# Loading the activation table set with exponential and logarithm in the output projection of a two-layer decoder kernel

## The chip, the cores and the metric

The kernel runs on one core of a Trainium2 chip (trn2). The metric is the device time of one execution in microseconds; the time before is the median of three runs.

## The reference

The reference is a decoder trunk of two layers on a sequence of 2048 real tokens with 16 learned meta tokens ahead of them, model width 1024, in float32. Every layer normalises, projects, attends, gates and projects back onto the residual stream.

```
for layer in range(2):
    hn = rmsnorm(h, norm_g[layer])
    if layer == 0:   # stick-breaking attention (8 heads) beside latent attention (8 heads)
        h = h + concat(o_sb * silu(g_sb), o_mla * silu(g_mla)) @ ev_w_out
    else:            # sliding window of 128, 16 heads, sinks and ALiBi
        h = h + (o * silu(g)) @ od_w_out
return rmsnorm(h, final_g)[:, 128:]
```

Here `rmsnorm(x, g)` is `x * rsqrt(mean(x*x) + 1e-6) * g`, and `silu(g)` is `g / (1 + exp(-g))`. The attention of layer 0 needs log-sigmoid, exponential and softmax; that of layer 1 a softmax with a sink.

## The kernel before, in words

Everything is one function, `build`, of a single program without loops on the device. It lays the sequence out as 17 blocks of 122 rows. Large products are made exact by splitting both factors into a rounded high part (float32r) and the remainder; every product is then three matmuls. A split is two instructions: a rounding copy on ACT or DVE, and a subtraction on POOL or DVE.

The work has these stages, by the time at which the profile shows them:

1. Norm and input projections of layer 0, up to about 600 us. The norm's reciprocal root is `rstd` (line 411): a logarithm on ACT (line 412) and an exponential of -0.5 times it (line 413). The gates are `silu` (line 435): on ACT an exponential (438), a logarithm (439) and an exponential (440).
2. The attention of layer 0, to about 1562 us. Its activations on ACT are Softplus (lines 1059, 1089, 1123) and Copy. The order of the instructions on PE, ACT, DVE and POOL is given by a planner (`list_schedule`).
3. The output projection of layer 0, from 1562 us. Here the order on PE, ACT, DVE, POOL and SP is the order of the program's text (`manual_schedule`, entered at line 1230). It begins with three blocks of rows at once (lines 1328 to 1345): eight steps k, each of which loads and splits one slice of the attention's result (`split_og`, line 1263: high part on ACT at line 1267, remainder on POOL at line 1268) and one slice of the weights (`split_w0`, line 1253: high parts on DVE, remainders on POOL at odd k and on DVE at even k), and then runs 18 matmuls (`out_mm`, lines 1273 to 1275). Slices are loaded two steps ahead over SP's queue into two buffers. Then follow the other 14 blocks in a fixed order of slots (lines 1346 to 1381): `step` loads and splits two more slices of the attention's result per call, `add` adds the residual on DVE, `scale` (line 1289) squares on ACT and calls `rstd`, `turn` transposes on PE and `place` (line 1301) scales, splits and stores into the operand of the next layer.
4. The projections of layer 1 for keys, values and queries (lines 1464 to 1551), to about 2010 us.
5. The windowed attention of layer 1 (lines 1559 to 1890), again in the order of the text on PE, ACT, DVE and POOL. It goes through 76 units (19 blocks of 108 queries, two halves, two groups of heads): scores on PE (lines 1598, 1599), their eviction on DVE with the row maximum (`mx`, line 1602), exponentials on ACT (line 1613), the product with the reciprocal sum on POOL (1622), transposes on PE (1632) with evictions on ACT (1635) and DVE (1637), and the product with the values on PE (1646). Between these steps `fill` puts matmuls of two other works from a queue, as many as a credit allows: first the gates of layer 1 (`gates`, line 1682, with the splits of the next weights in `w1_part` at lines 1417 on ACT and 1418 on DVE), then the output projection of layer 1 (`project`, line 1795). A gate's evacuation `gate_evac` (line 1692) is spread over the next ticks: line 1696 on DVE, the three activations below on ACT, and the product of line 1704 on DVE, which frees the gate's PSUM tile. Three such tiles exist.
6. The last rows: the final norm in `final` (line 1827) and, for the last block, `square` and `final_last` (lines 1807 to 1825), which again call `rstd`.

```
 411      def rstd(ss, n, scale):
 412          S.activation(ss[:n], ss[:n], AF.Ln, bias=epst[:n], scale=scale)
 413          S.activation(ss[:n], ss[:n], AF.Exp, scale=-0.5)

1698              def s2():
1699                  S.activation(g1[:, :n], g1[:, :n], AF.Exp)
1700                  S.activation(g1[:, :n], g1[:, :n], AF.Ln, bias=1.0)
1701                  S.activation(g1[:, :n], g1[:, :n], AF.Exp, scale=-1.0)
```

ACT takes its functions from the table set that is loaded. The first statement of `build`, line 370, loads one by name, `natural_log_exp_and_others`. Otherwise the text says nothing of tables: the loads that an activation needs are put in front of it when the program is built, and the profile shows each as an `ACT_TABLE_LOAD` on that activation's line.

Of the kernel before, what the change touches and what calls it, by code (L numbers as in the profile page):

```python
# [340 lines left out]
def build(tc, a, off, upto=99):  # L341
    nc = tc.nc
    V, S, G, T = nc.vector, nc.scalar, nc.gpsimd, nc.tensor
# [60 lines left out]
    def f(t):  # L404
        return t.bitcast(F32)

    def split(hi, lo, src, heng=None, leng=None):
        (heng or V).tensor_copy(hi, src)  # L408
        (leng or G).tensor_tensor(lo, src, f(hi), op=ALU.subtract)  # L409
# [816 lines left out]
    def part(c0):  # L1226
        return (*xA, 0) if c0 < HALF else (*xB, HALF)
# [11 lines left out]
    def load_x(b):  # L1239
        xt = xts[b] = tmp.tile([P, D], F32, tag="xt", name="xt")  # L1240
        if b == 0:
            G.memset(xt[0:32], 0.0)
            dma(xt[PAD:PAD + NMETA], a["meta"])
            dma(xt[PAD + NMETA:BK], a["x"][0, 0:BK - PAD - NMETA])
        else:
            r = b * BK - PAD - NMETA
            dma(xt[:BK], a["x"][0, r:r + BK])

    def load_w0(k):
        raws["w", k] = tmp.tile([P, D], F32, tag="xt", name="raw")  # L1250
        dma(raws["w", k], wout[:, k])

    def split_w0(k):
        raw = raws.pop(("w", k))
        for j in range(2):
            split(*wo[j][k], raw[:, 512 * j:512 * (j + 1)], leng=(G if k % 2 else V))

    def load_og(g, k):
        n = (QG[g][1] - QG[g][0]) * BK
        raws[g, k] = tmp.tile([P, 512], F32, tag="raw", name="raw")[:, :n]  # L1260
        dma(raws[g, k], d_og[g][:, k])

    def split_og(g, k):
        c0, c1 = QG[g][0] * BK, QG[g][1] * BK
        h, l, o = part(c0)
        raw, h, l = raws.pop((g, k)), h[:, k, c0 - o:c1 - o], l[:, k, c0 - o:c1 - o]
        S.activation(h, raw, AF.Copy)
        G.tensor_tensor(l, raw, f(h), op=ALU.subtract)

    def out_mm(b, j, k):  # L1270
        h, l, o = part(b * BK)
        r, ps = slice(b * BK - o, (b + 1) * BK - o), pss[b][:, j]
        T.matmul(ps[:BK], h[:, k, r], wo[j][k][0], start=(k == 0), stop=False)
        T.matmul(ps[:BK], h[:, k, r], wo[j][k][1], start=False, stop=False)
        T.matmul(ps[:BK], l[:, k, r], wo[j][k][0], start=False, stop=(k == KT - 1))
# [56 lines left out]
        pss[b] = ps_v.tile([P, 2, 512], F32, tag="o", name="pso")  # L1332
    for k in range(KT):
        split_og(4, k)
        split_w0(k)
        if k + 2 < KT:
            load_og(4, k + 2)
            load_w0(k + 2)
        else:
            loaded.append(pieces.pop(0))  # L1340
            load_og(*loaded[-1])
            load_x(first[k + 2 - KT])
        for b in first:
            for j in range(2):
                out_mm(b, j, k)
# [574 lines left out]
```

## Time and profile before

| | |
|---|---|
| median of 3 runs | 2607.51 us (2605.27 to 2611.18) |
| the profiled execution | 2609.1 us, its span 2607.3 us |
| mean granted clock of PE | 0.99 |
| PE busy | 2541.9 us, 97% of the span |
| ACT busy | 1492.2 us, 57% |
| DVE busy | 1533.2 us, 59% |
| POOL busy | 1038.9 us, 40% |
| DMA, share of 16 engines on the main queue | 45.3% |

The span is the time from the first to the last instruction of the profiled execution; its time is a little longer. PE is TensorE's matmuls and PEld its weight loads, which overlap; ACT is ScalarE, DVE VectorE, POOL GpSimd, SP the engine that issues most DMAs. Busy time is that of instructions; a matmul's end is modelled, so a busy PE is not PE at its peak. A view of waits names an instruction, behind an arrow the one that released it, and then the us waited in total, how often, and the longest. In a list of instructions in order of time each line has the start in us, the duration in us, engine, line and what it writes from what; idle time in front of it, with its releaser, stands in brackets. The granted clock is the share of full speed that PE was allowed.

### The profile page before, as it was taken

How to read it: one execution, taken by the hardware profiler on the slowest of the kernel's cores; microseconds unless marked ns; L12 is line 12 of the kernel's file. 1: busy time of each engine (PE TensorE's matmuls, PEld its weight loads, DVE VectorE, ACT ScalarE, POOL GpSimd, SP SyncE). 2: the span in 40 equal slices, each digit the busy share in tenths (PEclk: the TensorE clock that was granted, in tenths of full speed). 3: DMA queues.
4: the chain of work that ended last, by engine and by line, in shares of the span. 5: the costliest groups of instructions: out<-in, count | busy, mean ns of one | idle time of the engine just before them, and what ended most of it. 6: DMA issues, size and time to landing. Idle time of an engine off the chain costs nothing. (4 is left out here: it accounts for less than half of the span.)

```text
span 2607.3 us, 38925 instructions
## 1 busy us (share of the span) xinstructions
PE 2541.9 (97%) x13105; PEld 1975.7 (76%) x13105; DVE 1533.2 (59%) x3356; ACT 1492.2 (57%) x3492; POOL 1038.9 (40%) x846
## 2 busy tenths in 40 slices
PE   9999999999999999999999999999999899999998
PEld 7888988899966666666665657788999788767776
DVE  5365496778335665565575664333222576888984
ACT  6542121213268878878878773644222999976564
POOL 1011201000068778878878775200000223445551
PEclk9999999999999999999999999999999999999999
DMA  5476734342594352261331115526454444666653
GB/s 146 111 200 178 205 95 117 90 123 68 138 196 107 87 141 67 71 155 47 81 95 36 49 55 168 150 85 161 119 123 118 107 118 126 166 188 191 200 150 100
DMA packets 337858, 321.30 MB, mean 123 GB/s; under 512 B 143670, under 2 KB 319738, under 8 KB 337075
## 3 DMA queue, kind: packets, MB, share of 16 engines
q1 hardware_dynamic: 336939, 317.56, 45.3%
q8 instruction: 103, 1.69, 0.3%
q10 hardware_dynamic: 720, 1.26, 0.1%
q14 instruction: 96, 0.79, 0.1%
HBM read 198.28 MB, written 120.80 MB: 122 GB/s over the span
## 5 line engine op out<-in xcount | busy, mean ns | idle before, releaser
L1622 POOL TENSOR_TENSOR s_sb<-s_sb,den 108x1008 f32<-108x1008 f32 (+1 forms) x76 | 147.6, 1942 | 548.7 <-DVE den L1621 456.0
L1079 POOL TENSOR_TENSOR l<-sp,h 123x488 fp32r<-123x488 f32 (+3 forms) x253 | 294.0, 1168 | 109.0 <-DVE h L1074 88.3
L1074 DVE CAST h<-sp 123x488 fp32r<-123x488 f32 (+3 forms) x266 | 177.7, 673 | 258.5 <-ACT sp L1066 232.8
L1137 POOL TENSOR_TENSOR acc<-acc,p 122x488 f32<-122x488 f32 (+3 forms) x288 | 313.4, 1108 | 31.4 <-DVE p L1129 24.2
L419 PE MATMUL psd<-xh,wh 128*128 128x366 f32 (+1 forms) x760 | 274.2, 361 | 0.0
L420 PE MATMUL psd<-xl,wh 128*128 128x366 f32 (+1 forms) x760 | 267.8, 352 | 0.0
L421 PE MATMUL psd<-xh,wl 128*128 128x366 f32 (+1 forms) x760 | 267.8, 352 | 0.0
L1059 ACT ACTIVATE sp<-zp 123x488 f32<-123x488 f32 (+3 forms) x360 | 173.1, 515 | 63.7 <-PE zp L1048 30.9
L1089 ACT ACTIVATE a<-zp 123x488 f32<-123x488 f32 (+3 forms) x360 | 168.2, 503 | 40.7 <-PE zp L1085 24.0
L1066 ACT ACTIVATE sp<-zp 1x488 f32<-1x488 f32 (+3 forms) x320 | 154.3, 496 | 40.3 <-PE zp L1085 36.3
L1613 ACT ACTIVATE s_sb<-s_sb,nm 108x252 f32<-108x252 f32 (+1 forms) x304 | 149.2, 494 | 36.7 <-DVE nm L1604 36.7
L1123 ACT ACTIVATE p<-ms 122x488 f32<-122x488 f32 (+3 forms) x320 | 150.6, 513 | 23.6 <-PE mav L1145 21.3
L420 PEld LDWEIGHTS psd<-xl,wh 128*128 128x128 f32 x760 | 144.1, 190 | 15.9 <-issue 0.9
L419 PEld LDWEIGHTS psd<-xh,wh 128*128 128x128 f32 x760 | 144.0, 190 | 12.5 <-issue 0.7
L421 PEld LDWEIGHTS psd<-xh,wl 128*128 128x128 f32 x760 | 143.5, 189 | 10.9
L1047 PEld LDWEIGHTS zp<-q,kbig 128*123 128x123 f32 x320 | 58.9, 184 | 113.1 <-ACT a L1089 60.5
L1145 PE MATMUL mav<-p,mvbig 122*64 122x488 f32 (+3 forms) x640 | 142.8, 524 | 0.0
L1097 PE MATMUL av<-a,vbig 123*64 123x488 f32 (+3 forms) x640 | 142.4, 523 | 0.0
L1079 DVE TENSOR_TENSOR l<-sp,h 123x488 fp32r<-123x488 f32 (+3 forms) x107 | 131.4, 1234 | 16.8 <-ACT h L1072 13.2
L409 POOL TENSOR_TENSOR wl<-raw,wh 128x1024 fp32r<-128x1024 f32 x17 | 40.9, 2404 | 244.9 <-DVE wh L408 159.0
L1047 PE MATMUL zp<-q,kbig 128*123 128x488 f32 (+3 forms) x320 | 127.3, 401 | 8.5 <-DMA kbig<-d_sk 5.2
L1602 DVE CUSTOM_DVE_ANT_0 s_sb<-pss,bt,sinks 108x252 f32<-108x252 f32 (+1 forms) x304 | 127.3, 473 | 12.2 <-PE pss L1599 4.3
(518 smaller groups left out, 6995.4 us busy)
## 6 DMA issues: line engine op xcount, KB each, us to landing
kbig<-d_sk SPq DMA_DIRECT2D x32, 492.0 KB
q<-d_q SPq DMA_DIRECT2D x36, 432.0 KB
xt<-in_x SPq DMA_DIRECT2D x32, 448.0 KB
raw<-in_od_w_in SPq DMA_DIRECT2D x48, 256.0 KB
mq<-d_mq SPq DMA_DIRECT2D x32, 373.6 KB
raw<-in_ev_w_in SPq DMA_DIRECT2D x19, 512.0 KB
kkb<-d_kk SPq DMA_DIRECT2D x18, 472.0 KB
xt<-d_h SPq DMA_DIRECT2D x16, 512.0 KB
```

Source lines behind the costliest of these rows:

```text
L419: T.matmul(o, wh[:, k, m0:m1], xh[:, k, c0:c1], start=(k == 0), stop=False)
L420: T.matmul(o, wh[:, k, m0:m1], xl[:, k, c0:c1], start=False, stop=False)
L421: T.matmul(o, wl[:, k, m0:m1], xh[:, k, c0:c1], start=False, stop=(k == k_n - 1))
L1047: T.matmul(zp[:BC, :s.ns], k[:, 2 * m, c], q, start=True, stop=False)
L1059: S.activation(sp[:BC, :s.ns], s.zp[m][:BC, :s.ns], AF.Softplus)
L1066: S.activation(s.sp[m][0:1, n - k:n], s.prev.zp[m][0:1, :k], AF.Copy, scale=-1.0 / CW)
L1074: V.tensor_copy(h[:BC, :n], sp[:BC, :n])
L1079: on_(on).tensor_tensor(l[:BC, :n], s.sp[m][:BC, :n], f(s.h[m][:BC, :n]), op=ALU.subtract)
L1089: S.activation(x[:BC, :s.ns], s.zp[m][:BC, :s.ns], AF.Softplus)
L1123: S.activation(pt[:BK, :s.nm], s.ms[m][:BK, :s.nm], AF.Softplus, scale=MSC)
L1137: eng.tensor_tensor(g.acc[m][:BK, s.jm:g.n], g.acc[m][:BK, s.jm:g.n], s.pt[m][:BK, :n], op=ALU.add)
L1613: S.activation(s_sb[:nq, hh, :ww], s_sb[:nq, hh, :ww], AF.Exp, bias=nm[:nq, hh:hh + 1], scale=SLOPES[h], accum_out=den[:nq, hh:hh + 1])
```

## The change

One statement is put into the first loop of the output projection. Behind ACT's first split of the attention's result (k = 0) and ahead of the second, ACT loads the same table set as at line 370.

```
     for k in range(KT):
         split_og(4, k)
+        if k == 0:
+            S.preload_act_table_set("natural_log_exp_and_others")
         split_w0(k)
         if k + 2 < KT:
             load_og(4, k + 2)
```

The loop is that of line 1333. ACT's order is given by the text there, so the load stands behind line 1267 of k = 0 and in front of line 1267 of k = 1; `split_w0` has no work on ACT. The attention's Softplus instructions all stand ahead of it.

More of the change, by code (lines that the diff above doesn't have):

```diff
@@ L1334, in build @@
         split_og(4, k)
+        if k == 0:
+            S.preload_act_table_set("natural_log_exp_and_others")
         split_w0(k)
```

## The prediction

> **What bounds the kernel now.** I began with the groups of instructions on ACT, since the change concerns ACT's tables.
>
> ```profile
> L1700 ACT ACT_TABLE_LOAD x40 | 51.3, 1283 | 0.7
> L1701 ACT ACT_TABLE_LOAD x40 | 51.3, 1283 | 0.7
> ...
> L412 ACT ACT_TABLE_LOAD x33 | 42.3, 1283 | 0.6
> L413 ACT ACT_TABLE_LOAD x33 | 42.3, 1283 | 0.6
> ...
> L412 ACT ACTIVATE ss<-ss,epst 122x1 f32<-122x1 f32 (+1 forms) x50 | 14.8, 295 | 0.9
> ...
> L370 ACT ACT_TABLE_LOAD x1 | 1.3, 1283 | 0.7 <-PEq L1907 0.7
> ```
>
> Columns are the count, the busy time in us, the mean ns of one, and the idle time before. This is the finding on which all else rests: the program does not load a table once after the attention, it loads one 146 times (40+40+33+33). Line 412 is the logarithm and line 413 the exponential of the norm; lines 1700 and 1701 are the logarithm and second exponential of the gate. A load before the logarithm and another before the exponential of each pair means that the two functions come from two different sets in turn. Yet line 412 ran 50 times with 33 loads: the other 17 are the norms of stage one, behind the load of line 370, which names the combined set. There the pairs run without any load. So the combined set holds what those pairs need, and it is lost once, when the attention's Softplus takes another set.
>
> Next I cut the span into stretches, to see where PE falls short.
>
> ```profile
> 1562.00:1600.00 38.00, 35.32 (x145) 27.53 (x146) 21.68 (x29) 6.01 (x10) 24.67 (x18) 0.96 0.61 193
> 1600.00:1660.00 60.00, 56.34 (x264) 44.26 (x263) 20.79 (x37) 40.44 (x65) 20.92 (x18) 0.97 0.57 162
> 1660.00:2000.00 340.00, 339.57 (x1764) 301.00 (x1763) 101.27 (x218) 116.92 (x237) 9.21 (x14) 1.00 0.47 123
> ```
> ```profile
> 2013.00:2335.00 322.00, 301.42 (x1803) 251.29 (x1802) 237.35 (x810) 306.25 (x752) 103.55 (x52) 0.97 0.52 134
> 2335.00:2545.00 210.00, 209.64 (x1176) 161.98 (x1175) 184.45 (x466) 124.12 (x372) 116.68 (x55) 1.00 0.64 187
> ```
>
> After the stretch and its length stand the busy times of PE, PEld, DVE, ACT and POOL, then PE's granted clock. PE bounds the kernel: from 1660 to 2000 and from 2335 to 2545 it has no room at all. Two stretches are different. From 2013 to 2335 run the windowed attention and the gates together; PE lacks 20.6 us (322 - 301.4) and has a clock of 0.97, and there ACT is 95% busy (306.25 of 322). From 1600 to 1660, the first blocks of the output projection, PE lacks 3.7 us, also at 0.97. All 80 gate loads lie in the first of these stretches:
>
> ```profile
> L1701 ACT ACT_TABLE_LOAD  x40: 1283/1283/1283, 2022.6 to 2331.6; - x40
> ```
>
> **Who makes PE wait in the gate stage.** First PE's own waits between 2008 and 2397, then, over nearly the same stretch, those of DVE:
>
> ```profile
> PE psg L1682 <- DVE sl L1704: 10.4, 7, 2.8
> PE pss L1598 <- DVE mx L1602: 4.9, 4, 2.2
> PE pt L1632 <- DVE ptsb L1637: 2.8, 4, 1.2
> PE pt L1632 <- ACT ptsb L1635: 2.0, 2, 1.6
> ```
> ```profile
> DVE wl L1418 <- ACT wh L1417: 48.7, 21, 5.5
> ...
> DVE sl L1704 <- ACT sl L1701: 25.4, 19, 2.8
> ```
>
> PE names DVE, but DVE waits for ACT. The product of line 1704, which frees the gate's PSUM tile, comes behind ACT's Exp, Ln, Exp (25.4 us waited); the split of line 1418 waits 48.7 us for ACT's half of it, and the score and transpose evictions queue behind it on DVE. ACT is the engine that is late.
>
> A wait costs PE more than its idle time:
>
> ```profile
> 2216.85 0.38 PE L1682 MATMUL psg<-bl,wh 128*128 128x488 f32 x1
> 2217.07 0.39 PE L1682 MATMUL psg<-bh,wl 128*128 128x488 f32 x1
> 2219.63 0.37 PE L1598 MATMUL pss<-kkb,q 128*108 128x252 f32 x1 [2.17 <-DVE mx L1602]
> ...
> 2221.08 0.61 PE L1682 MATMUL psg<-bh,wh 128*128 128x488 f32 x1
> 2221.49 0.61 PE L1682 MATMUL psg<-bl,wh 128*128 128x488 f32 x1
> ...
> 2224.31 0.39 PE L1682 MATMUL psg<-bh,wl 128*128 128x488 f32 x1
> ```
>
> Before the wait, matmuls start 0.22 us apart; afterwards 0.41 us apart, until 2224.3. This slow spell is what the 0.97 stands for. Also, a matmul's modelled duration (0.39) runs past the start of the next (0.22), so each wait is about 0.17 us longer than the idle time says.
>
> **The change part by part.** The *removed loads* need a price. First a pair with loads, in the output projection, then one of stage one without:
>
> ```profile
> 1601.34 1.28 ACT L412 ACT_TABLE_LOAD   x1
> ...
> 1602.95 1.28 ACT L413 ACT_TABLE_LOAD   x1
> ...
> 1604.35 1.01 ACT L1292 ACTIVATE pso<-xt 122x1024 f32<-122x1024 f32 x1
> ```
> ```profile
> 102.31 0.30 ACT L412 ACTIVATE ss<-ss,epst 122x1 f32<-122x1 f32 x1
> 102.64 0.20 ACT L413 ACTIVATE ss<-ss 122x1 f32<-122x1 f32 x1
> 102.75 0.58 ACT L628 ACTIVATE vt<-psv 122x512 f32<-122x512 f32 x1
> ```
>
> From the first load to ACT's next work pass 3.01 us with loads, 0.44 us without: 2.57 us per pair, 1.28 per load. With the combined set in place from ACT's second split on, and nothing behind it that needs another set (Copy, Square, Exp and Ln all ran behind line 370), all 146 loads go: some 188 us of ACT's time. Most of it is hidden; what counts is where ACT held PE.
>
> The Trainium skill, "ScalarE: Activation LUTs", section "What ACT_TABLE_LOAD costs", counts a drain of 1380 ns beside the 1283 ns of the load, 2.66 us for every switch; by that an estimate of ACT's relief would be 388 us. The trace agrees on 1283 and shows no such drain, since a pair with two loads gives back 2.57 us and not 5.3.
>
> *Gate stage.* The time lost against a PE without waits: 20.6 us idle, 3% of 322 us = 9.7 us of clock, and the 17 waits of the four rows at 0.17 us = 2.9 us; 33.2 us together. ACT loses 80 loads of 1.28 us, 102 us of its 306, and would be busy for about 204 us in a stage of 292 us, 70%. I take as gone with ACT's lateness the whole of the waits for the gate's product and for ACT itself (10.4 + 2.0), and two thirds of the remaining 8.2 us, which DVE ends: 17.9 of 20.6 us, 87%. The share for clock and hidden waits goes along, as each hangs on a wait: 0.87 x 33.2 = 28.9 us. Next late there is PE itself, then DVE: with 237 us of 292 it would be 81% busy, and from 2335 to 2545 it is 88% busy (184.45 of 210) while PE misses 0.4 us in all. Bounds: nothing but the direct 12.4 us, or all of 33.2.
>
> *Output projection.* PE's waits from 1600 to 1660 that ACT causes, directly or through POOL, which takes the rest of the same split:
>
> ```profile
> PE pso L1273 <- ACT bh L1267: 0.9, 1, 0.9
> PE pso L1275 <- POOL bl L1268: 0.8, 2, 0.6
> ```
>
> The two norms at 1600 put four loads ahead of the next splits; these come 5.1 us earlier, and the DMAs that refill their two buffers, issued on SP, start earlier by as much. Lost are 3.7 us and 3% of 60 us, 5.5 us in all; I take 80%, 4.4 us (bounds 1.7 and 5.5). From 1660 to 2000 the loads cost PE nothing, so nothing is gained.
>
> *Tail.* After the last matmul there is no cover:
>
> ```profile
> 2599.77 0.16 DVE L1820 TENSOR_TENSOR ss<-ss 128x1 f32<-128x1 f32 x1
> 2601.05 0.29 ACT L412 ACTIVATE ss<-ss,epst 128x1 f32<-128x1 f32 x1
> ...
> 2602.65 0.20 ACT L413 ACTIVATE ss<-ss 128x1 f32<-128x1 f32 x1
> 2602.89 0.72 ACT L1823 ACTIVATE yt<-spare,ss 128x512 f32<-128x512 f32 x1
> ```
>
> The sum of squares is ready at 2599.93. Without loads the logarithm starts about 0.05 us later (the same hand-over, 2602.85 to 2602.89, takes 0.04), the exponential 0.33 us behind, the scaling 0.24 us behind that: 2600.55 instead of 2602.89, 2.3 us.
>
> *Added load.* One load of 1.28 us stands between the first and second split. Behind it are queued ACT's other splits, POOL's halves and PE's second group of matmuls:
>
> ```profile
> 1562.97 1.11 ACT L1267 ACTIVATE bh<-raw 128x488 fp32r<-128x488 f32 x2 [2.60 <-DVE wo00h L408]
> ```
> ```profile
> 1563.66 3.05 POOL L1268 TENSOR_TENSOR bl<-raw,bh 128x488 fp32r<-128x488 f32 x2 [1.71 <-ACT bh L1267]
> ...
> 1568.10 1.28 POOL L409 TENSOR_TENSOR wo11l<-raw,wo11h 128x512 fp32r<-128x512 f32 x1
> ```
> ```profile
> 1570.77 0.39 PE L1273 MATMUL pso<-wo01h,bh 128*122 128x512 f32 x1
> ```
>
> The second split ends at 1564.1 and would end at 1565.4. POOL finishes its two halves at 1566.7 and the weights of that step at 1569.4; even with the whole 1.3 us passed on it is done at 1570.7, as PE's second step starts at 1570.77. Cover: the 18 matmuls of the first step. Cost 0; without that cover 1.3 us.
>
> Sum: 28.9 + 4.4 + 2.3 - 0 = 35.6 us. The profiled execution took 2609.1 us (span 2607.3), which gives 2573.5; the median of the runs shown, 2607.5, lies 1.6 below it, so I say **2572**.
>
> **The rivals.** *DVE takes ACT's place* in the gate stage. For it: three of PE's four rows of waits name DVE, and the weight splits come in bursts of eight. Against: the 88% stretch without loss. Only the direct 12.4 us would be won, with their 60% share (12.4 of 20.6) of the 12.6 us for clock and hidden waits, 7.6: 2609.1 - 20.0 - 4.4 - 2.3 = 2582.4; at the lower bound, without that share, 2590.
>
> *The clock does not come back.* The slow spells would not belong to waits of this length. Then only idle time is won, 17.9 + 3.0 + 2.3 = 23.2: 2585.9. The row at 2219.63, with a wait of 2.17 us and the slow spell right behind it, speaks against. The Trainium skill, "TensorE: Matmul & The Clock Gate", section "What's actually happening", lets the clock fall only after an idle window of about 3.4 us, and no wait listed above is that long; by that rule this rival would be the forecast, and the trace does not agree.
>
> *The denser stage is granted less clock*, the case that ends slower. The work from 2013 to 2335 at full clock is 301.4 x 0.97 = 292.4 us; with 6.7 us won elsewhere, the kernel is slower than before once that stage takes over 328.7 us, at a clock under 0.89. At 0.85 it would take 344.0 us, and the kernel 2624. Against it stand 340 and 210 us with a full PE at 1.00.
>
> *The change does not hold the set*: the program still alternates, and one hidden load comes on top: 2609.1, or 2610.4 uncovered; in terms of the median 2607.5. Stage one speaks against it.
>
> **How the numbers follow.** Forecast 0.72, DVE 0.12, clock not regained 0.09, set not held 0.04, denser clock 0.03. A difference of 0.2% (5.2 us) is about what a measurement of this kernel can tell. The first three are faster, 0.93; the fourth same, 0.04; the fifth slower, 0.03. The forecast's own range comes from its bounds: all 33.2 + 5.5 + 2.3 = 41.0 us won gives 2568.1, in terms of the median 2566.5, and the 2.2 us by which the lowest run shown lies under the median 2564; at the other end 20 us in the gate stage, 1.7 in the projection and 2.3 in the tail give 2585. The range is 2564 to 2588: it takes in the clock rival and half of DVE's, and leaves out the rest.
>
> **What would show it.** In the changed profile: two table loads besides that of line 370 (Softplus, and the new one near 1563.5), none at lines 412, 413, 1700, 1701; ACT's busy time some 186 us lower (145 x 1.283); PE's clock 0.99 or 1.00 through the gate stage, and that stage about 29 us shorter; in the tail, about 0.3 us from the logarithm to the exponential; PE's second step at the start no later than now, counted from its first. I am wrong if loads remain at those lines, if PE still waits over 10 us for line 1704, or if waits for DVE's lines 1602 and 1637 grow.

## The result, and the profile after

The changed kernel takes 2569.85 us (median of 4 runs, 2568.74 to 2571.17) against 2606.42 us before (median of 4, 2605.27 to 2611.18): a ratio of 0.9855, 95% interval 0.9843 to 0.9867, 36.6 us less. The forecast was 2572, with a range from 2564 to 2588. The profiled execution took 2570.5 us, its span 2568.7 us, against 2609.1 and 2607.3. Of the runs below one, of gate_loads_a, took 3556.41 us at a mean granted clock of 0.64, and its median leaves it out.

In the groups of ACT these are the only lines with table loads that are left:

```profile
L370 ACT ACT_TABLE_LOAD x1 | 1.3, 1283 | 0.7 <-PEq L1909 0.7
L1059 ACT ACT_TABLE_LOAD x1 | 1.3, 1283 | 0.0
L1336 ACT ACT_TABLE_LOAD x1 | 1.3, 1283 | 0.0
```

One at the start, one for Softplus, and the new one: 146 loads have become one. (Behind line 1335 the changed kernel's numbers are two higher: 1706 is 1704 of before.) Next the first blocks of the output projection, by stretch, with the columns as before; and the stage of attention and gates, which here runs from 2001 to 2288:

```profile
1600.00:1660.00 60.00, 59.26 (x284) 47.38 (x283) 23.30 (x40) 29.05 (x61) 24.20 (x21) 1.00 0.62 181
```
```profile
2001.00:2288.00 287.00, 285.06 (x1784) 243.99 (x1783) 237.09 (x790) 204.09 (x657) 98.89 (x50) 1.00 0.55 141
```

PE lacks 0.7 us in the first where it lacked 3.7, and 1.9 us in the second where it lacked 20.6 in a stretch of 322; the granted clock is 1.00 in both, where it was 0.97. The stretch of before that goes, like the second, from the first score to the last gate matmul is a little shorter than the one of the prediction:

```profile
2008.00:2323.00 315.00, 297.39 (x1789) 249.44 (x1789) 228.04 (x784) 295.59 (x731) 97.84 (x49) 0.98 0.50 128
```

There PE lacked 17.6 us at a clock of 0.98; the other 3.0 us of the 20.6 lay behind the gates. ACT has 204 us of work in the gate stage, 71%, where it was busy for 94 to 95%. What PE still waits for between 1990 and 2360, and then, from 1970 on, DVE's wait for ACT's half of the weight splits:

```profile
PE pss L1600 <- DVE mx L1604: 1.9, 1, 1.9
PE psg L1684 <- DVE sl L1706: 1.3, 1, 1.3
PE psg L1684 <- DVE st L1548: 0.7, 1, 0.7
PE pso L1797 <- DVE wl L1770: 0.2, 1, 0.2
```
```profile
DVE wl L1420 <- ACT wh L1419: 15.6, 10, 3.0
```

The gate's tile is waited for once (1.3 us) and not seven times (10.4 us); DVE's wait for ACT's half of the split fell from 48.7 to 15.6 us (12.6 from 1990 on, in the stage itself). DVE's wait for the gate's last exponential (25.4 us) is no longer among its waits.

Where the time came from is read best by landmarks. Each is the first or last start of a line's matmuls in that line's own view, here the scores and the gates before, and then after:

```profile
L1598 PE MATMUL pss<-kkb,q x304: 273/279/547, 2008.3 to 2547.9; 128*108 128x252 f32 x144, 128*104 128x248 f32 x8
```
```profile
L1682 PE MATMUL psg<-bh,wl x128: 377/383/608, 2177.9 to 2322.5; 128*128 128x488 f32 x128
```
```profile
L1600 PE MATMUL pss<-kkb,q x304: 272/279/372, 2001.0 to 2511.6; 128*108 128x252 f32 x144, 128*104 128x248 f32 x8
```
```profile
L1684 PE MATMUL psg<-bh,wl x128: 377/383/470, 2151.1 to 2288.1; 128*128 128x488 f32 x128
```

From the first score to the last gate matmul passed 314.2 us (2322.5 - 2008.3), and now 287.1. The table gives the same legs for every kernel that was run, each from one profiled execution, in us. Leg 1 goes from the first matmul of the output projection to the first score, leg 2 to the last gate matmul, leg 3 to the last matmul of all, leg 4 to the end of the span.

| kernel | leg 1 | leg 2 | leg 3 | leg 4 |
|---|---|---|---|---|
| before | 444.7 | 314.2 | 275.4 | 9.4 |
| changed | 438.3 | 287.1 | 273.5 | 7.1 |
| gate_loads | 438.3 | 313.9 | 274.8 | 7.1 |
| gate_work | 438.4 | 316.2 | 275.5 | 7.1 |
| gate_loads_half | 439.1 | 291.7 | 273.6 | 7.2 |
| gate_loads_a | 438.0 | 306.2 | 274.0 | 7.2 |
| norm_loads | 445.7 | 287.1 | 271.7 | 9.5 |
| late_set | 444.7 | 288.4 | 274.2 | 7.1 |
| four_loads | 440.6 | 287.1 | 273.7 | 7.1 |
| tail_loads | 438.2 | 287.1 | 272.9 | 9.5 |

Won are 6.4, 27.1, 1.9 and 2.3 us. The rest of the 38.6 us between the two profiled spans, 0.9 us, lies ahead of the first leg, where nothing was changed: that landmark stands anywhere from 1559.6 to 1563.6 in these ten executions, so it is scatter.

### The profile page after: what moved, and what is told of

It is laid out like the page before. It is cut to its first block, busy times and chain, and to the rows that moved or that the text cites. A ratio compares the mean times of both kernels' runs of the same rounds, so it can differ in the third digit from the quotient of the medians.

```text
span 2568.7 us, 38780 instructions
## 1 busy us (share of the span) xinstructions
PE 2528.3 (98%) x13105; PEld 1969.7 (77%) x13105; DVE 1525.3 (59%) x3356; ACT 1313.7 (51%) x3347; POOL 1043.3 (41%) x846
## 3 DMA queue, kind: packets, MB, share of 16 engines
q10 hardware_dynamic: 720, 1.26, 0.1%
## 4 chain that ended last, share of the span: by engine, by line
PE 92%; DMA 3%; DVE 2%; SPq 1%; ACT 1%; issue 1%; POOL 1%; ACTq 0%; DVEq 0%; POOLq 0%
PE psd L419 8%; PE psd L420 8%; PE psd L421 8%; PE pso L1797 7%; PE psg L1684 7%; PE av L1097 5%; PE mav L1145 5%; PE zp L1047 4%; PE psx L967 3%; PE zp L1085 3%; PE zp L1084 3%; PE zp L1048 3%; PE ms L1117 3%; PE ms L1118 2%; PE pso L1273 2%; PE pso L1275 2%
## 5 line engine op out<-in xcount | busy, mean ns | idle before, releaser
L1066 ACT ACTIVATE sp<-zp 1x488 f32<-1x488 f32 (+3 forms) x320 | 154.3, 496 | 40.5 <-PE zp L1085 36.6
L1079 DVE TENSOR_TENSOR l<-sp,h 123x488 fp32r<-123x488 f32 (+3 forms) x107 | 132.4, 1243 | 16.9 <-ACT h L1072 13.3
```

What stands on the lines that cost most here:

```text
L1079: on_(on).tensor_tensor(l[:BC, :n], s.sp[m][:BC, :n], f(s.h[m][:BC, :n]), op=ALU.subtract)
```

## The experiments

The theory to be tested: the price of a load is ACT's time, paid only where PE waits for ACT; it is high in the gate stage, because ACT is full there, and small in the projection and the tail; the place of the new load is free. The rivals: the switch of tables costs by itself; every load costs alike; the shares do not add up. The experiments were measured apart from the result, beside medians of 2607.67 us (gate_loads, norm_loads, gate_work, late_set) and 2606.62 us (the others) for the kernel before. With that and the intervals, a difference to the changed kernel is good to about 5 us; what is smaller rests on the legs.

**gate_loads**: the loads are put back in the gates alone.

```
             S.activation(g1[:, :n], g1[:, :n], AF.Exp)
+            S.preload_act_table_set("natural_log")
             S.activation(g1[:, :n], g1[:, :n], AF.Ln, bias=1.0)
+            S.preload_act_table_set("natural_log_exp_and_others")
             S.activation(g1[:, :n], g1[:, :n], AF.Exp, scale=-1.0)
```

> The changed kernel with two table loads put back into every gate (80 loads: one set ahead of the logarithm, the combined set ahead of the second exponential), none in the norms. My theory: the gate stage's loss of about 29 us comes back, because ACT is again 95% busy there: 2570 + 29 = 2599 us (2594 to 2603), granted clock near 0.97 in that stage. Rival, the loads of norms and gates only hurt together: about 2570 + 15 = 2585 us.

Measured: 2598.62 us (ratio to before 0.9967, 0.9954 to 0.998). Leg 2 is back at 313.9 us. Its stretch, and PE's longest waits there:

```profile
1999.00:2313.00 314.00, 296.44 (x1785) 248.84 (x1784) 227.68 (x782) 295.06 (x730) 97.82 (x49) 0.98 0.50 128
```
```profile
PE psg L1684 <- DVE sl L1708: 10.3, 7, 2.8
```

ACT is 94% busy again (295.06 of 314), PE lacks 17.6 us, and the seven waits for a gate's tile are there with 10.3 us. The 80 loads of the gates hold 28.8 us (2598.62 - 2569.85) by themselves.

**norm_loads**: the same two statements in `rstd`, around the logarithm, behind the attention only; none in the gates.

> The changed kernel with two table loads put back into each of the 33 norms behind the attention (66 loads), none in the gates. My theory: only the projection's first blocks (5.6 us by the two traces) and the tail (2.4 us) come back: 2570 + 8 = 2578 us (2575 to 2580). Rival, every load costs alike (36.6 us over 145 loads, 0.25 us each): 2570 + 16.7 = 2587 us.

Measured: 2578.73 us (0.989, 0.9875 to 0.9905), 8.9 us over the changed kernel; leg 1 and leg 4 are those of before within 1 us, leg 2 that of the changed kernel. 28.8 + 8.9 = 37.7 us against 36.6 won: the shares add up within the noise, and the loads do not cost alike. A load cost 0.36 us in the gates (28.8 / 80) and 0.13 us in the norms (8.9 / 66), out of 1.28 us of ACT's time.

**gate_work**: no loads, but as much of ACT's time.

```
             S.activation(g1[:, :n], g1[:, :n], AF.Exp)
+            for _ in range(2 if n > 400 else 3):
+                S.activation(g1[:, :n], g1[:, :n], AF.Copy)
             S.activation(g1[:, :n], g1[:, :n], AF.Ln, bias=1.0)
+            for _ in range(2):
+                S.activation(g1[:, :n], g1[:, :n], AF.Copy)
             S.activation(g1[:, :n], g1[:, :n], AF.Exp, scale=-1.0)
```

> The changed kernel without any load in the gates, but with four (488 wide) or five (360 and 356 wide) copies of the gate onto itself on ACT, about 2.5 us per gate, as much as the two loads took. My theory, ACT's time is the price: as with the loads, 2599 us (2592 to 2605). Rival, the switch of tables itself costs (its traffic, or something it stops beside ACT): 2570 to 2574 us.

Measured: 2601.67 us (0.9978, 0.9967 to 0.9989). One gate on ACT, and PE's longest wait:

```profile
2196.77 0.60 ACT L1701 ACTIVATE sl<-sl 128x488 f32<-128x488 f32 x1
2197.40 1.26 ACT L1703 ACTIVATE sl<-sl 128x488 f32<-128x488 f32 x2
2198.69 0.61 ACT L1704 ACTIVATE sl<-sl 128x488 f32<-128x488 f32 x1
2199.34 1.26 ACT L1706 ACTIVATE sl<-sl 128x488 f32<-128x488 f32 x2
2200.62 0.61 ACT L1707 ACTIVATE sl<-sl 128x488 f32<-128x488 f32 x1
```
```profile
PE psg L1684 <- DVE sl L1710: 13.7, 11, 3.0
```

Two copies take 1.26 us, about as long as a load (1.28), and no table is switched; the loss returns whole. It is made up a little differently: PE lacks 22.3 us in leg 2, at a clock of 0.99, where it lacked 17.6 at 0.98 with the loads. So no price of the tables beside ACT's time shows here. The Trainium skill, "ScalarE: Activation LUTs", section "What ACT_TABLE_LOAD costs", adds a drain of about 1.38 us to each load; had there been one, the loads would have cost visibly more than these copies, and they cost 3 us less (2598.62 against 2601.67), which is within the noise. The runs do not agree with it, in this kernel.

**gate_loads_half**: the loads of gate_loads only in every second gate.

```
+            state["gate"] = state.get("gate", 0) + 1
+            odd = state["gate"] % 2
...
+                if odd:
+                    S.preload_act_table_set("natural_log")
```

> The changed kernel with the two loads put back into every second gate (40 loads). My theory, a queue on ACT: at 204 + 51 = 255 us of work in a stage of some 292 us ACT has room to catch up between gates, so less than half of the loss returns: 2570 + 6 = 2576 us (2573 to 2580). Rival, each load delays PE by its own share: half of 29 us, 2584.5 us.

Measured: 2575.23 us (0.9881, 0.9865 to 0.9898), 5.4 us over the changed kernel where a share by count would be 14.4.

```profile
2000.00:2292.00 292.00, 287.03 (x1786) 243.92 (x1784) 236.38 (x786) 250.37 (x693) 98.14 (x49) 1.00 0.54 137
```

At 86% (250.37 of 292) ACT can still catch up between gates. The loss behaves as that of a queue, steep near full: the first 40 loads cost 5.4 us (4.6 in leg 2), the other 40 cost 23.4.

**gate_loads_a**: the loads only `if x0 + n + R0 <= HALF`, in the gates of the first half of the sequence.

> The changed kernel with the two loads put back only into the 24 gates of the first half of the sequence (360 and 356 wide, 48 loads). My theory: by the trace of before PE's waits for a free gate tile lie nearly all in this half, where a gate takes less time on PE (24 matmuls 0.165 us apart) and so brings its loads more often; about two thirds of the loss return: 2570 + 19 = 2589 us (2585 to 2593). Rival, backlog carried from the first half into the second makes the second half's share: near the full 29 us, 2597 us.

Measured: 2586.76 us (median of three, 2586.70 to 2595.94; 0.9936, 0.9914 to 0.9958), 16.9 us over the changed kernel and within the range given. In two stretches:

```profile
1998.00:2145.00 147.00, 134.07 (x849) 119.03 (x847) 94.79 (x350) 137.16 (x333) 33.99 (x18) 0.97 0.43 110
2145.00:2304.00 159.00, 158.64 (x937) 128.42 (x933) 137.88 (x441) 125.73 (x373) 64.86 (x32) 1.00 0.61 154
```

The loads run from 2010 to 2178, those of 19 of the 24 gates in the first stretch. There lie PE's 12.9 us of lack and its low clock (ACT 93% busy). In the second stretch PE lacks 0.4 us, all of it ahead of 2178, while the last five gates still have their loads; behind them it is full. No backlog is carried on. That a load costs more in the first half is less sure: by the median these 60% of the loads bring 59% of the 28.8 us, and only leg 2 shows a larger share (19.1 of the 26.8 us that all 80 bring there, 71%).

**late_set**: the kernel before, with the set loaded behind the first unit's exponentials of the windowed attention.

```
             S.activation(se[:nq], se[:nq], AF.Exp)
+            if u == units[0]:
+                S.preload_act_table_set("natural_log_exp_and_others")
```

> The kernel before, with the one load of the combined set only behind the first unit of exponentials of the windowed attention, some 440 us later than in the change; the 17 norms ahead of it keep their 34 loads. My theory: all but the output projection's share is won: 2570 + 5.6 = 2575.5 us (2573 to 2578). Rival, the projection's earlier lead was given back later, at the start of the windowed attention: 2570 to 2571 us.

Measured: 2577.23 us (0.9885, 0.9871 to 0.99), 7.4 us over the changed kernel: 1.7 more than expected, within the range given. Leg 1 is that of before, 444.7 us, though the same to 0.1 us only by chance, as the last section shows. What the projection wins early is not given back later.

**four_loads**: four loads, of two sets in turn, at the place of the new one.

> The changed kernel with four loads instead of one behind ACT's first split of the output projection. My theory: the cover of about 1.4 us on POOL's way (PE's second step) is used up by three more loads of 1.3 us; PE waits some 1.8 us at the start of its second step, perhaps with a slow spell behind it: 2 to 3.5 us over the changed kernel. Rival, the cover is longer, since the later slices wait for DMA anyway: under 0.5 us.

Measured in one run: leg 1 is 440.6 us, 2.3 us longer than in the changed kernel (its time of 2572.7 us fits, but a single run can't tell that much). PE in the first steps:

```profile
1569.38 0.39 PE L1273 MATMUL pso<-wo01h,bh 128*122 128x512 f32 x1
1571.32 0.49 PE L1274 MATMUL pso<-wo01l,bh 128*122 128x512 f32 x1 [1.55 <-POOL wo01l L409]
1571.65 0.39 PE L1275 MATMUL pso<-wo01h,bl 128*122 128x512 f32 x1
1571.88 0.40 PE L1273 MATMUL pso<-wo11h,bh 128*122 128x512 f32 x1
1572.74 0.49 PE L1274 MATMUL pso<-wo11l,bh 128*122 128x512 f32 x1 [0.47 <-POOL wo11l L409]
```

PE waits twice, 1.55 and 0.47 us, on POOL's way as worked out. The cover of the one load was real, and three more use it up.

**tail_loads**: the two loads only in `final_last`.

> The changed kernel with two loads put back into the very last norm alone. My theory: 2.4 us from the last matmul to the end come back (7.1 to 9.5 us in the trace), all else equal. Rival, the last output's transfer hides a part of it: under 1 us.

Measured in one run: leg 4 is 9.5 us and not 7.1.

```profile
2562.99 1.28 ACT L1823 ACT_TABLE_LOAD   x1
2563.01 0.16 DVE L1822 TENSOR_TENSOR ss<-ss 128x1 f32<-128x1 f32 x1
2564.29 0.29 ACT L1824 ACTIVATE ss<-ss,epst 128x1 f32<-128x1 f32 x1
2564.60 1.28 ACT L1825 ACT_TABLE_LOAD   x1
2565.89 0.20 ACT L1826 ACTIVATE ss<-ss 128x1 f32<-128x1 f32 x1
```

The first load covers DVE's sum, ready after 0.18 us; the rest of both loads is on the path.

## Why the prediction was right, point by point

**The loads go.** Right: one new load, none left at the norms and gates. ACT's busy time fell by 178.5 us (1492.2 to 1313.7), less than the 186 forecast. The durations of ACT's instructions, added up over all groups of the two profiles, fell by 184.3 us (1648.3 to 1464.0). Busy time counts instructions that overlap only once, so most of the gap is overlap that was there before and is not after.

**Gate stage, 28.9 us forecast.** The loads of the gates hold 28.8 us. Of the 27.1 us that leg 2 won, 15.7 are idle time (17.6 to 1.9) and 11.4 are clock and hidden waits. The forecast had 17.9 and 11.0, with the 3.0 us behind the gates among the idle time; so both terms hold, and not only their sum. Leg 3 won another 1.9 us, but it lies between 271.7 and 274.2 us among the kernels without loads in the gates, so how much of that is the loads' is not shown. The reading that mattered was to follow PE's waits, which name DVE, one step further to what DVE waits for. DVE did not take ACT's place: it is 83% busy (237.09 of 287), and PE lacks 1.9 us in the stage.

**Output projection, 4.4 us forecast (1.7 to 5.5).** Undersized: leg 1 won 6.4 us. Until its last matmul the projection won 5.6 (214.0 us from its first matmul before, 208.4 after), just over my upper bound. Two steps failed. The first is the size: I took 80% of idle time and clock, and no hidden part of the waits, which I had counted in the gate stage. Between 1600 and 1660 these waits of PE stood beside the two of the prediction, and the last two lines are all that is left after:

```profile
PE nt L1299 <- issue: 1.0, 2, 0.6
PE nt L1299 <- DMA raw<-d_og: 0.6, 1, 0.6
PE pso L1273 <- DVE rs L1308: 0.4, 1, 0.4
```
```profile
PE pso L1273 <- DVE rs L1308: 0.4, 1, 0.4
PE nt L1299 <- issue: 0.4, 1, 0.4
```

Five of seven waits went, the one for DMA among them: 3.0 us of idle time (3.7 to 0.7), 1.8 us of clock (3% of 60), and, as an estimate at 0.17 us for each wait, 0.9 us hidden, 5.7 together. The second step is "From 1660 to 2000 the loads cost PE nothing". Before, the norms of the last two blocks stood ahead of the first weight splits of layer 1 on ACT, and PE waited for these between 1776 and 1800:

```profile
1777.02 1.28 ACT L413 ACT_TABLE_LOAD   x1
1778.31 0.20 ACT L413 ACTIVATE ss<-ss 122x1 f32<-122x1 f32 x1
1778.42 2.44 ACT L1417 ACTIVATE wh<-raw,gT 128x128 fp32r<-128x128 f32 x8
```
```profile
PE psd L419 <- ACT wh L1417: 0.4, 1, 0.4
```

A stretch of 340 us in which PE lacked 0.4 us had that wait in it, and the changed kernel has no wait there. From the projection's last matmul to the first score 0.8 us were won, the remainder of the 6.4; 0.4 of them are this wait's idle time, and where the rest lay was not tried.

**Tail, 2.3 us forecast.** Right: 2.3 in the profile. The changed kernel's last norm:

```profile
2563.54 0.16 DVE L1822 TENSOR_TENSOR ss<-ss 128x1 f32<-128x1 f32 x1
2563.73 0.29 ACT L412 ACTIVATE ss<-ss,epst 128x1 f32<-128x1 f32 x1 [0.22 <-DVE ss L1822]
2564.06 0.20 ACT L413 ACTIVATE ss<-ss 128x1 f32<-128x1 f32 x1
2564.29 0.72 ACT L1825 ACTIVATE yt<-spare,ss 128x512 f32<-128x512 f32 x1
```

The logarithm follows the sum by 0.03 us, the exponential the logarithm by 0.33 us, as in stage one.

**Added load, 0 us forecast.** Right. ACT, then PE at its first and its second step:

```profile
1562.08 0.61 ACT L1267 ACTIVATE bh<-raw 128x488 fp32r<-128x488 f32 x1 [2.60 <-DVE wo00h L408]
1562.71 1.28 ACT L1336 ACT_TABLE_LOAD   x1
1564.01 0.61 ACT L1267 ACTIVATE bh<-raw 128x488 fp32r<-128x488 f32 x1
```
```profile
1562.74 0.49 PE L1273 MATMUL pso<-wo00h,bh 128*122 128x512 f32 x1 [2.18 <-ACT bh L1267]
...
1569.87 0.40 PE L1273 MATMUL pso<-wo01h,bh 128*122 128x512 f32 x1
```

7.13 us lie between the steps, as before (1563.64 to 1570.77).

**The clock.** The forecast counted the slow spells as part of the waits, and the clock did come back, to 1.00. But that each wait has its spell went too far, as the last section shows, and so did "right behind it": after the wait that ends at 2219.63 the matmuls run at full pace for another 1.2 us, and the slow spell lasts from 2220.9 to 2224.3. The stage at full density was not granted less.

## What to carry to other kernels

Count the table loads in the profile before looking at anything else on ACT: two functions that alternate can be served by two sets in turn although one set holds both, and a set that was named at the start is lost with the first function from outside it. A load costs what ACT's time costs at that place: nothing where ACT has room, about 0.3 to 0.6 us each where it is full, and nearly all of it in a tail without cover. When PE waits for DVE, ask what DVE waits for.

## What the runs showed of the hardware that was not expected

The same lack of PE did not always bring a slow clock. In the first blocks of the projection, with the same loads in place, norm_loads and then late_set show:

```profile
1600.00:1660.00 60.00, 56.00 (x260) 43.69 (x259) 21.08 (x37) 40.33 (x66) 20.93 (x18) 0.97 0.55 162
```
```profile
1600.00:1660.00 60.00, 55.90 (x264) 43.51 (x264) 22.16 (x39) 41.26 (x68) 21.19 (x19) 1.00 0.56 166
```

Both lack 4.0 to 4.1 us, one at a clock of 0.97 and one at 1.00; and the wait of 1.55 us in four_loads has matmuls 0.23 us apart right behind it, while that of 2.17 us before had them 0.41 us apart from 1.2 us behind it on. In the stretch ahead, from 1562 to 1600, all these kernels begin with the same two waits (2.18 and 1.04 us), and the clock there is 0.96 before and in four_loads but 0.91 in norm_loads and late_set. Such spells alone move leg 1 by up to some 2 us (5% of 38 us, 3% of 60). The Trainium skill, "TensorE: Matmul & The Clock Gate", section "What's actually happening", describes a window of about 3.4 us that runs freely beside the program; that would let the same wait meet it or miss it, which agrees with these rows. That it takes a whole idle window, as the page also says, does not agree with a slow spell behind 2.17 us. Which waits bring a spell was not tried and stays open.
